# Weight rows moved by 64 bytes, and sample tokens handled in blocks of heads, in a one-core decoder step

## The chip, the core and the metric

The kernel runs on one core of a Trainium2 chip. The metric is the device time of one execution in microseconds (us); the times of a kernel are several executions of it, and the profile is one more, taken by the hardware profiler. The engines are TensorE (matmuls; its weight loads have a row of their own in the profile, PEld), VectorE (DVE), ScalarE (ACT), GpSimd (POOL) and SyncE (SP), whose queue issues all DMA transfers here. The memory beside the engines is SBUF, 128 partitions of bytes; the matmuls write to PSUM, in banks.

## The reference

One layer of a hybrid decoder for 256 prompt tokens and 8 sample tokens (one new token of each of eight sequences), width 2048, all in float32:

```python
xn = rmsnorm(x, norm1_g)
z_u, z_v, q, k, v, g = split(xn @ w_in)              # 2048 x 6144, six parts of 1024 columns
z_v = layernorm(gelu(z_v), sgu_norm_g)               # 8 heads of 128 channels
out_a = gelu(z_u) * (tril(W_s) z_v + b)              # per head, over positions in chunks of 128
out_b = silu(g) * groupnorm(retention(rot(q), rot(k), v, state)) * ret_gn_g   # 8 heads of 128
h = x + concat(out_a, out_b) @ w_out
h = h + cross_attention(rmsnorm(h, norm2_g), memory) # w_cq; w_ck, w_cv of 256 memory tokens; w_co
h = h + relu(rmsnorm(h, norm3_g) @ w_ff1)**2 @ w_ff2 # 2048 -> 8192 -> 2048
y = rmsnorm(h, final_norm_g)
```

A sample token is alone in its chunk: its position mixing is one number per head, W_s[0, 0], and its bias is b[0]. Its retention reads and updates a stored 128 x 128 state per head. The outputs are y, the memory's keys and values, the retention states of prompt and samples, and the samples' layer-normed v.

## The kernel before

**Layout.** Activations lie transposed: 128 features on the partitions, 264 tokens (T; 8 samples first, then the prompt) along the free dimension. A float32 matmul is made of three matmuls in the type fp32r: each operand is split into a high part (a rounded copy) and a low part (the rest), and a product is high x high + high x low + low x high. In the profile the three are lines 163 (weights high, activation high), 164 (weights high, activation low) and 165 (weights low, activation high). These three in a row are called a triple here.

**Weights.** All weights come as chunks of 256 x 512 numbers, two rows of 128 x 512 side by side in one tile [128, 2, 512]; `chunks` is the list of them in order. For each chunk SP loads `w` (five buffers), ScalarE copies it to the high part `wh` (line 1071) and VectorE subtracts for the low part `wl` (line 1079), four buffers each, two chunks ahead of TensorE. Row k of the tile (0 "even", 1 "odd") begins k x 2048 bytes into it. `group_act` takes a chunk with four accumulators of 128 output columns (m) and both rows k: eight triples, 24 matmuls, with 264 columns of activations streaming (256 for `w_ck`, where the memory streams). `group_mem` (`w_cv`) has the roles exchanged: memory tokens as the loaded operand and 512 columns of weights streaming. `group_last` holds the last four chunks of `w_ff2`, sorted by m.

**Activation rows.** `rows` makes tiles [128, 2, 576] for four rows of 264 numbers, and `row(t, k)` finds row k at 272 x (k mod 2) columns, 1088 bytes, in half k // 2; halves are 2304 bytes apart. They sit in 26 slots ("s") of one size, 4608 bytes. The memory's operands are tiles [128, 4, 256] with rows of 1024 bytes.

**Order of work.** Everything else is written as generators. `run_point` is called after every two triples: it advances every `chain` that is due, then the first due task of `tasks` (one per point, with lanes that keep order), then issues due stores (`store`, ten points after the call unless said otherwise). The instructions of each engine stand in the order in which this emits them.

**Around the change.** The order of the input projection is v, q, k, q, k, v, vA, vA, g, g, u, u, with 8 chunks each. `retention(h)` runs for eight heads in two lanes: transposes of k and v, scores, the state product `pp` and its copy `so` (line 647, one buffer) with a store, ScalarE's scaling of the old sample states (line 649), and four steps on VectorE in which `st` is updated and multiplied with the queries into `rs_t` [128, 8] (lines 658 and 660). Then the prompt's products `rp` and a transpose of `rs_t` to 8 partitions, the group norm of both (`s1`, `s2`, cleared by two memsets on VectorE, lines 672 and 673, and filled by ScalarE's accumulating operations, lines 675 and 682), and three transposes back, one of them of the 8 sample rows. `spatial(h)` does the position mixing of a head: a matmul on 8 partitions with a small diagonal matrix `dg` for the samples (line 486), two on 128 partitions for the prompt (line 488), and VectorE's scaling and bias for each. `sample_attn` is the samples' cross-attention. The tag "t" has nine buffers of 264 numbers that many steps share (`t264`), "sm" 24 small ones, "ms" three PSUM banks (`misc`), "mm" five (`bank`).

Of the kernel before, what the change touches and what calls it, by code (L numbers as in the profile page):

```python
# [42 lines left out]
def _emit(tc, cst, wpool, spool, tpool, psum, dpool, I, O):  # L43
# [21 lines left out]

    def small(n, name):
        return tpool.tile([128, n], F32, name=name, tag="sm", bufs=24)
# [28 lines left out]
    w00 = cst.tile([8, 8], F32, name="w00")  # L96
# [24 lines left out]
    def group_last(w, opnd, evict):  # L121
        st = {}

        def mm(ci, hi, lo):
# [3 lines left out]
            for m in R4:  # L128
                ps = bank([128, T], "acc")
                for i in range(8):  # L130
                    xh, xl = opnd(i)
                    h, l = st[i // 2]
                    a = h[:, i % 2, m * 128:(m + 1) * 128]
                    b = l[:, i % 2, m * 128:(m + 1) * 128]
# [39 lines left out]
    def group_mem(w, opnd, evict):  # L174
        st = {}

        def mm(ci, hi, lo):
            if ci == 0:
                st["ps"] = [bank([128, 512], "acc") for _ in range(2)]
            for tq in range(2):  # L180
                for k in range(2):
# [5 lines left out]
                    pe.matmul(ps, lhsT=a, rhs=hi[:, k, :], start=(kt == 0), stop=False)  # L187
                    pe.matmul(ps, lhsT=a, rhs=lo[:, k, :], start=False, stop=False)  # L188
                    pe.matmul(ps, lhsT=b, rhs=hi[:, k, :], start=False, stop=(kt == 15))  # L189
# [182 lines left out]
    def sgu_loads():  # L372
# [5 lines left out]
        sp.dma_start(out=w00[:], in_=I["w00"].partition_broadcast(8))  # L378
# [36 lines left out]
    def ev_vA(g):  # L415
        def ev(ps):
            z = normed(ps)
            ge = slot([128, 4, T], "ge")
            if g == 0:
                sgu_loads()  # L420
                S["vn"] = [slot([128, 1024], "vn0"), slot([128, 1024], "vn1"), None]
                S["vns"] = slot([8, 1088], "vns")
                S["vn"][2] = S["vns"][:, 0:1024]
# [11 lines left out]
            def gen():  # L435
# [4 lines left out]
                else:  # L440
                    chain(layernorm(), 12)
                    for h in range(8):
# [29 lines left out]
    def masks():  # L472
        gp.tensor_tensor(out=S["wst"][:], in0=S["wst"][:], in1=trilt.unsqueeze(1).broadcast_to([128, 8, 128]),
                         op=ALU.mult)
        dg = S["vns"][:, 1024:1088].rearrange("p (h b) -> p h b", h=8)
        gp.tensor_tensor(out=dg, in0=ident[0:8, 0:8].unsqueeze(1).broadcast_to([8, 8, 8]),
                         in1=w00[:].unsqueeze(2).broadcast_to([8, 8, 8]), op=ALU.mult)
        S["dg"] = dg
        yield
        S["spat"] = [slot([128, 4, T], "spat") for _ in range(2)]  # L480

    def spatial(h):
        vn = S["vn"]
        c = slice(h * 128, (h + 1) * 128)
        ps = misc([128, T], "spp")
        pe.matmul(ps[:, 0:8], lhsT=vn[2][:, c], rhs=S["dg"][:, h, :], start=True, stop=True)
        for q in range(2):
            pe.matmul(ps[:, 8 + 128 * q:136 + 128 * q], lhsT=vn[q][:, c], rhs=S["wst"][:, h, :],  # L488
# [4 lines left out]
            in0=ps[:, 8:T].rearrange("p (q i) -> p q i", q=2), scalar=gain(G_SGU, h),  # L493
# [76 lines left out]
    def retentions(g):  # L570
        if g == 0:
            S["state"] = {}
            load_state(0)
            load_state(1)
        for h in range(4 * g, 4 * g + 4):
# [33 lines left out]
    def retention(h):  # L609
# [8 lines left out]
        kn = S["rpool"].tile([128, 384], F32, name="kn", tag="kn", bufs=2)  # L618
# [27 lines left out]
        so = S["rpool"].tile([128, 128], F32, name="so", tag="so", bufs=1)  # L646
        act.copy(so[:], pp[:])
        store(O["state_p"][h], so[:])
        act.activation(st[:], st[:], AF.Copy, scale=GAMMA[h])
        yield 2  # L650
        rs_t = S["rpool"].tile([128, 8], F32, name="rs_t", tag="rs_t", bufs=2)
# [11 lines left out]
        store(O["state_s"][h], st[:])  # L663
        yield 2
        rp = misc([128, 3, 128], "rp")
# [7 lines left out]
        dve.memset(s2[:], 0.0)  # L673
        for i, (c0, n) in enumerate(TOK):
            act.activation(rn[0:n, i * 128:(i + 1) * 128], rp[0:n, i, :], AF.Copy, accum_out=s1[0:n, i:i + 1])

        def norm():
            nm = small(3, "gnm")
            dve.tensor_scalar(out=nm[:], in0=s1[:], scalar1=-1.0 / 128, scalar2=None, op0=ALU.mult)
            yield 2  # L680
            for i, (c0, n) in enumerate(TOK):
                act.activation(jk[0:n, i * 128:(i + 1) * 128], rn[0:n, i * 128:(i + 1) * 128], AF.Square,
                               bias=nm[0:n, i:i + 1], accum_out=s2[0:n, i:i + 1])
            yield
            va, rs = small(3, "gva"), small(3, "grs")
            dve.tensor_scalar(out=va[:], in0=s2[:], scalar1=1.0 / 128, scalar2=EPS, op0=ALU.mult, op1=ALU.add)
            rsqrt(rs[:], va[:], 3)
            yield 2
            for i, (c0, n) in enumerate(TOK):
                y = rn[0:n, i * 128:(i + 1) * 128]  # L690
                dve.tensor_scalar(out=y, in0=y, scalar1=nm[0:n, i:i + 1], scalar2=rs[0:n, i:i + 1],
# [3 lines left out]
        tp = misc([128, T], "tp")  # L695
        for i, (c0, n) in enumerate(TOK):
            transpose(tp[:, c0:c0 + n], rn[0:n, i * 128:(i + 1) * 128])
        act.activation(vt, tp[:], AF.Copy, scale=halfgn[:, h:h + 1])
        done.add(h)

    def ev_g(g):
        def ev(ps):
# [3 lines left out]
            def gen():  # L706
# [4 lines left out]
                assert done.issuperset(range(4 * g, 4 * g + 4))  # L711
# [133 lines left out]
    def sample_attn(h):  # L845
# [6 lines left out]
        sc = small(16, "scs")  # L852
# [23 lines left out]
        so = S["mpool"].tile([128, 4, 8], F32, name="so", tag="so", bufs=4)  # L876
# [191 lines left out]
    def emit_hi(i):  # L1068
        hi = wpool.tile([128, 2, 512], F32R, name="wh", tag="wh", bufs=N_CAST)
        for k in (slice(0, 1), slice(1, 2)) if i < FINE else (slice(0, 2),):  # L1070
            act.copy(hi[:, k, :], raws[i][:, k, :])  # L1071
# [178 lines left out]
```

## Time and profile before

| | |
|---|---|
| median of 3 runs | 1579.33 us (1578.64 to 1582.74) |
| profiled execution, its own time | 1581.44 us |
| its span, first to last instruction | 1579.6 us |
| TensorE busy, matmuls | 1563.9 us, 12515 matmuls |
| VectorE busy | 1037.8 us |
| ScalarE busy | 747.9 us |
| GpSimd busy | 122.4 us |
| DMA | 334.61 MB, 212 GB/s in the mean |
| granted TensorE clock | 0.998 |

In rows of the profile, "L164 PE MATMUL acc<-rl,wh 128*128 128x264 f32 x128 | 36.0, 281" reads: line 164, TensorE, a matmul from tiles rl and wh into acc, 128 rows by 128 columns of weights, 264 columns streamed, 128 of them, 36.0 us busy in sum, 281 ns the mean of one. Matmuls overlap, so a matmul lasts longer than the interval to the next one's start. Rows in the order of time have start (us), length (us), and then the same; "[0.79 <-DVE ra L538]" is idle time before it and what ended it. Rows of waits have who waited for whom, the sum in us, how often, and the longest.

### The profile page before, as it was taken

The page shows a single profiled execution, that of the slowest core. Times are in us where ns is not written, and L with a number is a line of the kernel's source. Part 1 is how long each engine was busy: PE and PEld are TensorE (multiplying, and loading weights), DVE is VectorE, ACT ScalarE, POOL GpSimd, SP SyncE. Part 2 cuts the span into 40 slices and gives each one's busy share as a digit, 9 for nine tenths or more (in the row PEclk, how much of TensorE's full clock was granted, in tenths as well). Part 3 has the DMA queues.
Part 4 walks back from the last instruction along what each step waited for, and adds up shares of the span by engine and source line. Part 5 has one row for each costly group of instructions (what it writes and reads, how often), then busy time and mean ns, then how long its engine had stood idle before and what let it go on. Part 6 is the DMA issues. An engine that isn't in the chain of part 4 may idle for free.

```text
span 1579.6 us, 30820 instructions
## 1 busy us (share of the span) xinstructions
PE 1563.9 (99%) x12515; PEld 1537.5 (97%) x12515; DVE 1037.8 (66%) x1875; ACT 747.9 (47%) x1165; POOL 122.4 (8%) x111
## 2 busy tenths in 40 slices
PE   9999999999999999999999999999999999999997
PEld 8999999999999998899999999999999999999997
DVE  6677688778668777876665555655555465555555
ACT  7445566357544444444454543534444343444443
POOL 0332122110011201010000000000000000000000
PEclk9999999999999999999999999999999999999999
DMA  7677876466578888876555555555655656555552
GB/s 288 193 269 257 281 238 204 154 190 228 185 259 312 298 282 294 310 250 249 182 180 187 183 177 188 174 188 173 189 185 176 190 171 192 179 185 187 171 187 88
DMA packets 98927, 334.61 MB, mean 212 GB/s; under 512 B 11152, under 2 KB 16336, under 8 KB 98784
## 3 DMA queue, kind: packets, MB, share of 16 engines
q1 hardware_dynamic: 98784, 332.64, 63.1%
q8 instruction: 98, 1.61, 0.4%
q14 instruction: 45, 0.37, 0.1%
HBM read 321.42 MB, written 11.17 MB: 211 GB/s over the span
## 4 chain that ended last, share of the span: by engine, by line
issue 47%; PE 47%; DVE 2%; DMA 2%; ACT 0%; SPq 0%; POOL 0%; DVEq 0%; ACTq 0%; POOLq 0%
PE acc L163 13%; PE acc L165 13%; PE acc L164 12%; PE acc L187 2%; PE acc L189 2%; PE acc L188 2%; DMA out_state_p_dram<-so 1%; DVE wl L1079 1%; DMA w<-in_w_in_dram 1%; PE tp L107 1%; PE qb L858 0%; DVE state L658 0%; DVE bkq L660 0%; PE spp L488 0%; DMA bkq<-kqd 0%
## 5 line engine op out<-in xcount | busy, mean ns | idle before, releaser
L1071 ACT CAST wh<-w 128x1024 fp32r<-128x1024 f32 (+1 forms) x513 | 536.0, 1046 | 683.4 <-PE acc L164 596.6
L1079 DVE TENSOR_TENSOR wl<-w,wh 128x1024 fp32r<-128x1024 f32 (+1 forms) x513 | 626.3, 1233 | 256.3 <-ACT wh L1071 255.7
L165 PE MATMUL acc<-h2h,wl 128*128 128x264 f32 x1024 | 290.9, 284 | 0.0
L163 PE MATMUL acc<-h2h,wh 128*128 128x264 f32 x1024 | 290.6, 284 | 0.0
L164 PE MATMUL acc<-h2l,wh 128*128 128x264 f32 x1024 | 288.1, 281 | 0.0
L165 PE MATMUL acc<-rh,wl 128*128 128x264 f32 x992 | 281.8, 284 | 0.0
L163 PE MATMUL acc<-rh,wh 128*128 128x264 f32 x992 | 281.3, 284 | 0.0
L164 PE MATMUL acc<-rl,wh 128*128 128x264 f32 x992 | 279.1, 281 | 0.0
L163 PE MATMUL acc<-xh,wh 128*128 128x264 f32 x768 | 224.9, 293 | 3.9 <-DVE vt L566 1.9
L165 PE MATMUL acc<-xh,wl 128*128 128x264 f32 x768 | 218.8, 285 | 0.4 <-DVE wl L1079 0.2
L164 PE MATMUL acc<-xl,wh 128*128 128x264 f32 x768 | 216.6, 282 | 0.1
L165 PEld LDWEIGHTS acc<-h2h,wl 128*128 128x128 f32 x1024 | 192.5, 188 | 0.0
L164 PEld LDWEIGHTS acc<-h2l,wh 128*128 128x128 f32 x1024 | 192.4, 188 | 0.0
L163 PEld LDWEIGHTS acc<-h2h,wh 128*128 128x128 f32 x1024 | 192.3, 188 | 0.0
L165 PEld LDWEIGHTS acc<-rh,wl 128*128 128x128 f32 x992 | 186.5, 188 | 0.0
L164 PEld LDWEIGHTS acc<-rl,wh 128*128 128x128 f32 x992 | 186.4, 188 | 0.0
L163 PEld LDWEIGHTS acc<-rh,wh 128*128 128x128 f32 x992 | 186.3, 188 | 0.0
L163 PEld LDWEIGHTS acc<-xh,wh 128*128 128x128 f32 x768 | 145.3, 189 | 5.9 <-DVE vt L566 2.1
L164 PEld LDWEIGHTS acc<-xl,wh 128*128 128x128 f32 x768 | 145.5, 189 | 0.3 <-DVE xl L115 0.3
L165 PEld LDWEIGHTS acc<-xh,wl 128*128 128x128 f32 x768 | 145.0, 189 | 0.9 <-DVE wl L1099 0.4
L989 DVE TENSOR_TENSOR hT<-hT,acc 128x264 f32<-128x264 f32 x124 | 53.2, 429 | 71.6 <-PE acc L165 71.6
L103 POOL TENSOR_TENSOR msr<-msv,neghalf 128x3 f32<-128x3 f32 (+1 forms) x5 | 7.8, 1561 | 975.9 <-DVE msv L279 731.8
(249 smaller groups left out, 2740.1 us busy)
## 6 DMA issues: line engine op xcount, KB each, us to landing
w<-in_w_ff_dram SPq DMA_DIRECT2D x256, 512.0 KB, 3.8
w<-in_w_in_dram SPq DMA_DIRECT2D x95, 512.0 KB, 4.1
w<-in_w_out_dram SPq DMA_DIRECT2D x32, 512.0 KB, 3.9
w<-in_w_cq_dram SPq DMA_DIRECT2D x32, 512.0 KB, 4.2
kv<-in_kN_dram SPq DMA_DIRECT2D x32, 512.0 KB, 5.3
kv<-in_vT_dram SPq DMA_DIRECT2D x32, 512.0 KB, 5.0
w<-in_w_ck_dram SPq DMA_DIRECT2D x32, 512.0 KB, 5.7
w<-in_w_cv_dram SPq DMA_DIRECT2D x32, 512.0 KB, 4.6
```

The source lines that it names most:

```text
L103: gp.tensor_tensor(out=out, in0=in_, in1=neghalf[0:in_.shape[0], 0:n], op=ALU.pow)
L107: pe.transpose(out, in_, ident[0:p, 0:p])
L163: pe.matmul(ps, lhsT=a, rhs=xh, start=(i == 0), stop=False)
L164: pe.matmul(ps, lhsT=a, rhs=xl, start=False, stop=False)
L165: pe.matmul(ps, lhsT=b, rhs=xh, start=False, stop=(i == nk - 1))
L187: pe.matmul(ps, lhsT=a, rhs=hi[:, k, :], start=(kt == 0), stop=False)
L188: pe.matmul(ps, lhsT=a, rhs=lo[:, k, :], start=False, stop=False)
L189: pe.matmul(ps, lhsT=b, rhs=hi[:, k, :], start=False, stop=(kt == 15))
L989: dve.tensor_tensor(out=h[m], in0=h[m], in1=ps[m][:], op=ALU.add)
L1071: act.copy(hi[:, k, :], raws[i][:, k, :])
L1079: dve.tensor_tensor(out=lo[:, k, :], in0=raw[:, k, :], in1=hi[:, k, :].bitcast(F32), op=ALU.subtract)
```

## The change

There are two parts.

1. The high and low weight tiles become [128, 1088] (`wcol`). Row k begins at column 528 k, 2112 bytes, so that the odd row begins 64 bytes further modulo 256 than before. The casts write both rows through one access pattern with a gap (`both`), the matmuls read `half_of(t, k)`. Raw tiles `w` and activation rows stay.
2. Sample tokens are taken out of the per-head steps. `spatial_s` transposes the eight heads' samples into one PSUM tile and scales and biases them in four VectorE operations, with `w00` now loaded to 128 partitions and multiplied by the gain; `spatial(h)` keeps the prompt alone. `sample_norm(g)` does the group norm of four heads' samples on 32 partitions, after the last of them; `retention(h)` keeps the prompt's two blocks. For room in SBUF `so` of retention moves to the "t" buffers, `scs` to buffers of its own, the result of `sample_attn` into `q8[h]`, and `kn` and `vns` shrink.

```diff
+    def wcol(name):
+        return wpool.tile([128, 1088], F32R, name=name, tag=name, bufs=N_CAST)
+
+    def half_of(t, k):
+        return t[:, 528 * k:528 * k + 512]
+
+    def both(t):
+        return t[:, 0:1056].rearrange("p (k f) -> p k f", k=2)[:, :, 0:512]
...
-                a = hi[:, k, m * 128:(m + 1) * 128]
-                b = lo[:, k, m * 128:(m + 1) * 128]
+                a = half_of(hi, k)[:, m * 128:(m + 1) * 128]
+                b = half_of(lo, k)[:, m * 128:(m + 1) * 128]
...
-        sp.dma_start(out=w00[:], in_=I["w00"].partition_broadcast(8))
+        sp.dma_start(out=w00[:], in_=I["w00"].partition_broadcast(128))
...
+                    defer(spatial_s(), 56)
                     for h in range(8):
                         defer(spatial(h), 56)
...
-        gp.tensor_tensor(out=dg, in0=ident[0:8, 0:8].unsqueeze(1).broadcast_to([8, 8, 8]),
-                         in1=w00[:].unsqueeze(2).broadcast_to([8, 8, 8]), op=ALU.mult)
-        S["dg"] = dg
+        gp.tensor_tensor(out=w00[:], in0=w00[:], in1=gcol[:, G_SGU:G_SGU + 8], op=ALU.mult)
...
+    def spatial_s():
+        ps = misc([128, 64], "sps")
+        for h in range(8):
+            transpose(ps[:, 8 * h:8 * h + 8], S["vn"][2][:, h * 128:(h + 1) * 128])
+        for g in range(2):
+            hs = slice(4 * g, 4 * g + 4)
+            o = S["spat"][g][:, :, 0:8]
+            dve.tensor_tensor(out=o, in0=ps[:, 32 * g:32 * g + 32].rearrange("p (h b) -> p h b", h=4),
+                              in1=w00[:, hs].unsqueeze(2).broadcast_to([128, 4, 8]), op=ALU.mult)
+            dve.tensor_tensor(out=o, in0=o, in1=S["bbc"][:, hs, 0:1].broadcast_to([128, 4, 8]), op=ALU.add)
+        yield
...
-        pe.matmul(ps[:, 0:8], lhsT=vn[2][:, c], rhs=S["dg"][:, h, :], start=True, stop=True)
...
-        dve.tensor_scalar(out=o[:, 0:8], in0=ps[:, 0:8], scalar1=gain(G_SGU, h),
-                          scalar2=S["bbc"][:, h, 0:1], op0=ALU.mult, op1=ALU.add)
...
-        so = S["rpool"].tile([128, 128], F32, name="so", tag="so", bufs=1)
-        act.copy(so[:], pp[:])
+        so = t264("so")[:, 0:128]
+        act.copy(so, pp[:])
...
+        S["left"][g] -= 1
+        if not S["left"][g]:
+            defer(sample_norm(g), 4)
...
-        transpose(rp[0:8, 2, :], rs_t[:])
...
-        s1, s2 = small(3, "gs1"), small(3, "gs2")
-        dve.memset(s1[:], 0.0)
-        dve.memset(s2[:], 0.0)
-        for i, (c0, n) in enumerate(TOK):
-            act.activation(rn[0:n, i * 128:(i + 1) * 128], rp[0:n, i, :], AF.Copy, accum_out=s1[0:n, i:i + 1])
+        s1, s2 = small(2, "gs1"), small(2, "gs2")
+        for i in range(2):
+            act.activation(rn[:, i * 128:(i + 1) * 128], rp[:, i, :], AF.Copy, accum_out=s1[:, i:i + 1])
...
-        tp = misc([128, T], "tp")
-        for i, (c0, n) in enumerate(TOK):
-            transpose(tp[:, c0:c0 + n], rn[0:n, i * 128:(i + 1) * 128])
-        act.activation(vt, tp[:], AF.Copy, scale=halfgn[:, h:h + 1])
+        tp = misc([128, 256], "tp")
+        for i in range(2):
+            transpose(tp[:, i * 128:(i + 1) * 128], rn[:, i * 128:(i + 1) * 128])
+        act.activation(vt[:, 8:T], tp[:], AF.Copy, scale=halfgn[:, h:h + 1])
...
+    def sample_norm(g):
+        rp = misc([32, 128], "rps")
+        transpose(rp[:], S["rs_t"][g][:])
+        x = half("rns")[0:32, 0:128]
+        s1, s2, nm, va, rs = [small(1, "gss")[0:32, :] for _ in range(5)]
+        act.activation(x, rp[:], AF.Copy, accum_out=s1)
...
+        chain(norm(), 2)
+        yield 16
+        tp = misc([128, 32], "tps")
+        transpose(tp[:], x)
+        dve.tensor_tensor(out=S["v"][g][:, :, 0:8], in0=tp[:].rearrange("p (m b) -> p m b", m=4),
+                          in1=halfgn[:, 4 * g:4 * g + 4].unsqueeze(2).broadcast_to([128, 4, 8]), op=ALU.mult)
+        done.add(8 + g)
...
-        so = S["mpool"].tile([128, 4, 8], F32, name="so", tag="so", bufs=4)
+        so = q8[h]
...
-        hi = wpool.tile([128, 2, 512], F32R, name="wh", tag="wh", bufs=N_CAST)
-        for k in (slice(0, 1), slice(1, 2)) if i < FINE else (slice(0, 2),):
-            act.copy(hi[:, k, :], raws[i][:, k, :])
+        hi = wcol("wh")
+        if i < FINE:
+            for k in range(2):
+                act.copy(half_of(hi, k), raws[i][:, k, :])
+        else:
+            act.copy(both(hi), raws[i][:])
```

`emit_lo` changes in the same way as `emit_hi`, and `group_last`, `group_mem` and the first chunk read and write through `half_of`.

More of the change, by code (lines that the diff above doesn't have):

```diff
@@ L95, in _emit @@
     sel = cst.tile([128, 8], F32R, name="sel")
-    w00 = cst.tile([8, 8], F32, name="w00")
+    w00 = cst.tile([128, 8], F32, name="w00")
     halfgn = cst.tile([128, 8], F32, name="halfgn")
@@ L186, in mm @@
                     ps = st["ps"][tq][:]
-                    pe.matmul(ps, lhsT=a, rhs=hi[:, k, :], start=(kt == 0), stop=False)
-                    pe.matmul(ps, lhsT=a, rhs=lo[:, k, :], start=False, stop=False)
-                    pe.matmul(ps, lhsT=b, rhs=hi[:, k, :], start=False, stop=(kt == 15))
+                    pe.matmul(ps, lhsT=a, rhs=half_of(hi, k), start=(kt == 0), stop=False)
+                    pe.matmul(ps, lhsT=a, rhs=half_of(lo, k), start=False, stop=False)
+                    pe.matmul(ps, lhsT=b, rhs=half_of(hi, k), start=False, stop=(kt == 15))
                     yield
@@ L484, in spatial @@
         c = slice(h * 128, (h + 1) * 128)
-        ps = misc([128, T], "spp")
-        pe.matmul(ps[:, 0:8], lhsT=vn[2][:, c], rhs=S["dg"][:, h, :], start=True, stop=True)
+        ps = misc([128, 256], "spp")
         for q in range(2):
-            pe.matmul(ps[:, 8 + 128 * q:136 + 128 * q], lhsT=vn[q][:, c], rhs=S["wst"][:, h, :],
+            pe.matmul(ps[:, 128 * q:128 * q + 128], lhsT=vn[q][:, c], rhs=S["wst"][:, h, :],
                       start=True, stop=True)
@@ L571, in retentions @@
         if g == 0:
-            S["state"] = {}
+            S["state"], S["rs_t"], S["left"] = {}, {}, {}
             load_state(0)
             load_state(1)
+        S["left"][g] = 4
         for h in range(4 * g, 4 * g + 4):
@@ L645, in retention @@
             pe.matmul(pp[:], lhsT=kn[:, c], rhs=vn[:, c], start=(i == 0), stop=(i == 1))
-        so = S["rpool"].tile([128, 128], F32, name="so", tag="so", bufs=1)
-        act.copy(so[:], pp[:])
-        store(O["state_p"][h], so[:])
+        so = t264("so")[:, 0:128]
+        act.copy(so, pp[:])
+        store(O["state_p"][h], so)
         act.activation(st[:], st[:], AF.Copy, scale=GAMMA[h])
         yield 2
-        rs_t = S["rpool"].tile([128, 8], F32, name="rs_t", tag="rs_t", bufs=2)
+        if g not in S["rs_t"]:
+            S["rs_t"][g] = S["rpool"].tile([128, 32], F32, name="rs_t", tag="rs_t", bufs=2)
+        rs_t = S["rs_t"][g][:, 8 * m:8 * m + 8]
         for b0 in range(0, 8, 2):
@@ L710, in gen @@
                 yield
-                assert done.issuperset(range(4 * g, 4 * g + 4))
+                assert done.issuperset([*range(4 * g, 4 * g + 4), 8 + g])
                 for m in R4:
@@ L1068, in emit_hi @@
     def emit_hi(i):
-        hi = wpool.tile([128, 2, 512], F32R, name="wh", tag="wh", bufs=N_CAST)
-        for k in (slice(0, 1), slice(1, 2)) if i < FINE else (slice(0, 2),):
-            act.copy(hi[:, k, :], raws[i][:, k, :])
+        hi = wcol("wh")
[4 more added lines that the diff above has]
+            act.copy(both(hi), raws[i][:])
         his[i] = hi
     def emit_lo(i):
-        lo = wpool.tile([128, 2, 512], F32R, name="wl", tag="wl", bufs=N_CAST)
+        lo = wcol("wl")
         hi = his.pop(i)
         raw = raws.pop(i)
-        for k in (slice(0, 1), slice(1, 2)) if i < FINE else (slice(0, 2),):
-            dve.tensor_tensor(out=lo[:, k, :], in0=raw[:, k, :], in1=hi[:, k, :].bitcast(F32), op=ALU.subtract)
+        if i < FINE:
+            for k in range(2):
+                dve.tensor_tensor(out=half_of(lo, k), in0=raw[:, k, :], in1=half_of(hi, k).bitcast(F32),
+                                  op=ALU.subtract)
+        else:
+            dve.tensor_tensor(out=both(lo), in0=raw[:], in1=both(hi).bitcast(F32), op=ALU.subtract)
         casts[i] = (hi, lo)
```

50 lines of the change are left out of this document (28 added, 22 removed).

## The prediction

> **What bounds the kernel now.** I read the page's first part, then busy time by stretches, then starts of single matmuls in the order of time, then the waits of each engine. TensorE has no slack: from 830 to 1555 us it is busy for the whole of the time, while VectorE and ScalarE work about half of it.
>
> ```profile
> PE 1563.9 (99%) x12515; PEld 1537.5 (97%) x12515; DVE 1037.8 (66%) x1875; ACT 747.9 (47%) x1165; POOL 122.4 (8%) x111
> ```
>
> ```profile
> 85.00:270.00 185.00, 181.64 (x1473) 178.34 (x1472) 146.29 (x390) 106.29 (x253) 43.67 (x40) 0.99 0.75 255
> 830.00:1555.00 725.00, 725.00 (x6017) 725.00 (x6016) 405.88 (x512) 314.88 (x396) 1.77 (x1) 1.00 0.56 181
> ```
>
> (Columns: length, then busy time and count of TensorE, its weight loads, VectorE, ScalarE, GpSimd, clock, DMA.) So whatever changes the interval from one matmul's start to the next, or puts fewer instructions on TensorE, moves the end one for one; what VectorE, ScalarE or a queue gains counts only where TensorE waits for it, and that is between 85 and 270 us.
>
> The interval is not the same everywhere. These are starts of the first matmul of a weight chunk at both ends of two undisturbed stretches, then the count of matmuls between (each count has the two that hang over the ends):
>
> ```profile
> 326.77 0.28 PE L163 MATMUL acc<-mgh,wh 128*128 128x264 f32 x1
> ...
> 372.85 0.28 PE L163 MATMUL acc<-mgh,wh 128*128 128x264 f32 x1
> ...
> 1045.34 0.28 PE L163 MATMUL acc<-rh,wh 128*128 128x264 f32 x1
> ...
> 1161.07 0.28 PE L163 MATMUL acc<-h2h,wh 128*128 128x264 f32 x1
> ```
>
> ```profile
> 326.77:372.85 46.08, 46.08 (x386) 1.00 0.67 221
> 1045.34:1161.07 115.73, 115.73 (x962) 1.00 0.57 183
> ```
>
> 46.08 us over 384 is 120.00 ns; 115.73 us over 960 is 120.55 ns. Both stretches run the same code with operands at the same places modulo 256. Which matmul has the excess shows in the length of the second matmul of a triple (L164), here of two successive triples at 1051 us, the even operand row and then the odd one:
>
> ```profile
> L164 PE MATMUL acc<-rl,wh 128*128 128x264 f32 x1 | 0.3, 279 | 0.0
> ```
>
> ```profile
> L164 PE MATMUL acc<-rl,wh 128*128 128x264 f32 x1 | 0.3, 284 | 0.0
> ```
>
> From 300 to 390 us both rows have the short one, 278 ns in the mean; from 1000 to 1090 us, where 279 and 284 alternate, it is 281:
>
> ```profile
> L164 PE MATMUL acc<-mgl,wh 128*128 128x264 f32 x96 | 26.7, 278 | 0.0
> ...
> L164 PE MATMUL acc<-mul,wh 128*128 128x264 f32 x80 | 22.3, 278 | 0.0
> ...
> L164 PE MATMUL acc<-xl,wh 128*128 128x264 f32 x75 | 20.9, 278 | 0.0
> ```
>
> ```profile
> L164 PE MATMUL acc<-rl,wh 128*128 128x264 f32 x128 | 36.0, 281 | 0.0
> ```
>
> The odd row begins 272 x 4 = 1088 bytes behind the even one, 64 modulo 256; its weights 2048 bytes behind, 0 modulo 256. The even row and its weights agree modulo 256, the odd ones don't. The excess falls on the odd row, as it must if the relation matters.
>
> **Part 1: the weight tiles.** Weights of odd rows move by 64 bytes. If the odd row then runs like the even one, six matmuls cost 720.0 instead of 723.3 ns. The chunk list has 448 chunks of 264 columns, 24 matmuls each: 10752. The 96 + 80 + 75 triples just shown, 753 matmuls, are at 120.00 already, so 10000 x 0.55 ns = 5.5 us. What loses: the memory operand has rows of 1024 bytes, all at an even place, so the odd weights of w_ck and w_cv stop agreeing with it: 128 + 64 pairs of rows x 3.3 ns = 0.6 us at the most, and nothing at the least, since 256 columns are fewer; I take 0.3. And each third matmul of a triple now runs while weights at the other row's place are loaded; its price isn't in the trace (the odd rows have it with all three), so bounds: nothing, or the odd row's whole excess again, which cancels the 5.5. I take nothing, because in the odd triple it is the second matmul that is long.
>
> One rule speaks against this part. The Trainium skill, TensorE: Matmul & The Clock Gate (Step-by-step: what each phase is for), says that TensorE reads weights and moving operand through two independent SBUF ports, so that loading the next weights takes nothing from the running matmul. By that rule the relation of the two addresses is worth 0. The trace agrees as far as 120.00 ns occurs with disagreeing addresses; it doesn't with the 279 and 284.
>
> The casts now write two runs of 512 with a gap, in one instruction still:
>
> ```profile
> L1071 ACT CAST wh<-w 128x1024 fp32r<-128x1024 f32 (+1 forms) x513 | 536.0, 1046 | 683.4 <-PE acc L164 596.6
> L1079 DVE TENSOR_TENSOR wl<-w,wh 128x1024 fp32r<-128x1024 f32 (+1 forms) x513 | 626.3, 1233 | 256.3 <-ACT wh L1071 255.7
> ```
>
> VectorE's is 1.23 us and ScalarE's 1.05 per chunk of 24 x 120.55 ns = 2.89 us; the trace has no such cast, so bounds: nothing, or as much again per run as half a cast, 0.6 us, which VectorE could still hide. I take nothing, being nearest to the same number of elements. VectorE is fullest from 85 to 270 us (146 of 185), and if that cover is gone, each late cast stops TensorE.
>
> **Part 2: sample tokens in blocks, on TensorE.** Instructions on 8 partitions are dear. A spatial head, against the retention product that has the same four passes:
>
> ```profile
> 291.62 0.28 PE L165 MATMUL acc<-xh,wl 128*128 128x264 f32 x1
> 291.84 0.38 PE L486 MATMUL spp<-vns 8*128 8x8 f32 x2
> 292.15 0.71 PE L488 MATMUL spp<-wst,vn 128*128 128x128 f32 x4
> ...
> 292.82 0.28 PE L164 MATMUL acc<-xl,wh 128*128 128x264 f32 x1
> ```
>
> ```profile
> 233.66 0.28 PE L165 MATMUL acc<-xh,wl 128*128 128x264 f32 x1
> 233.78 0.61 PE L645 MATMUL pp<-vn,kn 128*128 128x128 f32 x4
> ...
> 234.35 0.29 PE L164 MATMUL acc<-xl,wh 128*128 128x264 f32 x1
> ```
>
> 1.20 against 0.69 us: the 8-row product costs 0.51 us, eight times 4.1. The last transposes of a head, three with one on 8 rows, against a pair:
>
> ```profile
> 214.66 0.29 PE L165 MATMUL acc<-xh,wl 128*128 128x264 f32 x1
> 214.78 0.54 PE L107 MATMUL tp<-cmat,kn 128*128 128x128 f32 x3
> ...
> 215.48 0.29 PE L164 MATMUL acc<-xl,wh 128*128 128x264 f32 x1
> ```
>
> ```profile
> 217.42 0.28 PE L165 MATMUL acc<-xh,wl 128*128 128x264 f32 x1
> 217.54 0.38 PE L107 MATMUL tp<-cmat,k 128*128 128x128 f32 x2
> ...
> 217.88 0.28 PE L164 MATMUL acc<-xl,wh 128*128 128x264 f32 x1
> ```
>
> 0.82 against 0.46: 0.36 us, eight times 2.9. The pair itself is 0.46 less two intervals of 0.12, so a full-row transpose is 0.11; eight of rs_t go, 0.9. Added: sample_norm twice, a full-row transpose and one on 32 rows, which I price like 8 rows: 2 x 0.47 = 0.9. spatial_s, eight transposes on 8 rows: the first 0.36, each more the second pass of the spatial product, 0.51 - 0.36 = 0.15: 1.4 (between 0.4, were the seven free, and 2.9, were each a first). Net 4.1 + 2.9 + 0.9 - 0.9 - 1.4 = 5.6 us, bounds 4.1 to 6.6.
>
> **Part 2: waits.** Between 85 and 270 us TensorE stops three times:
>
> ```profile
> 130.90 0.28 PE L165 MATMUL acc<-xh,wl 128*128 128x264 f32 x1
> 131.97 0.39 PE L163 MATMUL acc<-xh,wh 128*128 128x264 f32 x1 [0.79 <-DVE ra L538]
> ...
> 159.82 0.28 PE L165 MATMUL acc<-xh,wl 128*128 128x264 f32 x1
> 161.96 0.47 PE L163 MATMUL acc<-xh,wh 128*128 128x264 f32 x1 [1.86 <-DVE vt L566]
> ```
>
> ```profile
> 199.59 0.28 PE L668 MATMUL rp<-vn,sm 128*128 128x128 f32 x1
> 200.56 0.27 PE L107 MATMUL rp<-cmat,rs_t 128*8 128x128 f32 x1 [0.70 <-DVE bkq L660]
> ```
>
> Less an ordinary interval these are 0.95, 2.02 and 0.86 us. Behind them stand ScalarE's waits:
>
> ```profile
> ACT kn L675 <- DVE gs L673: 20.8, 6, 5.2
> ...
> ACT so L647 <- DMA out_state_p_dram<-so: 12.3, 3, 5.8
> ```
>
> The first is for memsets of s1 and s2, queued on VectorE behind the state updates; they go, and the copy of z that the first stop needs is queued behind that wait. The third stop is the rs_t transpose, which leaves that place. The second stop's vt is queued behind state updates that ScalarE released late, after waiting for the store of so. so moves into the nine "t" buffers. Counted in order, the second pair of heads gets different buffers; in the first and third pair eight other tiles lie between, so the ninth is the same buffer again and that wait stays. All three stops lose their cause: 3.8 us. Bounds: 0, if VectorE is merely late elsewhere, to 3.8. Next late would be the ge transposes after the third pair's store. One wait is added: sample_norm's first transpose needs the last state update of four heads, and the weight matmuls queue behind it; it comes four points (2.9 us) later instead of two, so I take 0 for it, and at most 0.86 twice, as the third stop. VectorE also loses 16 memsets and 8-row operations, ScalarE 16 short ones; hidden, but in the fullest stage. w00 goes to 128 partitions instead of 8, one small load on SP's queue, needed a dozen points later; GpSimd's mask is as small as before. Both free.
>
> **The sum.** 5.5 - 0.3 + 5.6 + 3.8 = 14.6 us. The profiled execution took 1581.4 us (span 1579.6), 2.1 over the median of 1579.33; where it lost these 2.1 nothing shows. From the one 1566.8, from the other 1564.7; I say 1566.
>
> **Rivals.** (1) The places modulo 256 do nothing: both speeds occur with the same addresses, a matter of phase that settles at either. For it: the 120.00 ns stretch, and w_ck, where all places agree and L164 is no shorter than its neighbours:
>
> ```profile
> L164 PE MATMUL acc<-meml,wh 128*128 128x256 f32 x58 | 16.4, 283 | 0.0
> L163 PE MATMUL acc<-memh,wh 128*128 128x256 f32 x58 | 16.4, 283 | 0.0
> ```
>
> Against: odd and even differ steadily at 1051 us. Then 9.4 us less: 1571. By the Trainium skill's rule above this is the case. (2) Part 1 gives nothing and the stops merely move, ScalarE's store waits of the first and third pair still holding up casts: 5.6 less, 1575. Against it: two of the three causes are taken out, not shifted. (3) The price moves to the third matmul: in each of the 1792 pairs two matmuls run while weights 64 bytes off are loaded. If each lost the time of 64 bytes of moving row, 16 columns, by 120 ns / 264 that is 7.3 ns, 14.5 per pair less the 3.3 gained: 20 us, and 20 - 9.4 gives 1590, slower. It decides from 5.2 ns net per pair. Against it: today's odd rows have the offset on all three and pay 3.3 per pair.
>
> **Numbers.** The forecast has 0.52, its own range 1563 to 1569; rival 1 has 0.27, rival 2 0.13, rival 3 0.05, the rest 0.03 for waits in the new blocks. The range, 1562 to 1575, reaches through rival 1 to the edge of rival 2. A measurement here can tell 0.3%, 4.7 us: forecast, rival 1 and about half of rival 2 are faster by more, 0.86; 0.09 the same; 0.05 slower.
>
> **What would show it.** Right: chunk starts 2.880 us apart after 830 us, L164 at 278 to 279 ns in every group; no 8-row product at the spatial heads, bursts of 0.69 there; no wait of ScalarE for gs; TensorE busy throughout 85 to 270 us. Wrong: L164 still at 281 (rival 1); L165 or L163 longer (rival 3); stops with the same releasers at 131 or 160 us (rival 2).

## The result and the profile after

| | before | after |
|---|---|---|
| median | 1579.59 us (6 runs) | 1589.2 us (6 runs, 1586.58 to 1591.28) |
| ratio, 95% interval | | 1.0056, 1.0044 to 1.0069 |
| span of the profiled execution | 1579.6 us | 1589.0 us |
| forecast | | 1566 us, 1562 to 1575 |

The change makes the kernel 9 to 10 us slower. TensorE is as full as before; from 830 to 1555 us it only gets through fewer matmuls, 5935 where it was 6017. First the engine totals of the profile after, then busy time by stretches:

```profile
PE 1573.5 (99%) x12495; PEld 1548.5 (97%) x12495; DVE 1035.2 (65%) x1855; ACT 744.8 (47%) x1141; POOL 121.8 (8%) x113
```

```profile
85.00:270.00 185.00, 182.17 (x1476) 180.05 (x1475) 147.21 (x375) 105.65 (x230) 43.90 (x43) 0.99 0.76 257
830.00:1555.00 725.00, 725.00 (x5935) 725.00 (x5934) 399.37 (x503) 309.10 (x390) 1.77 (x1) 1.00 0.55 180
```

The lines 163, 164 and 165 of a triple are 172, 173 and 174 now. Starts of the first matmul of a chunk at both ends of two stretches of after, 29 and 40 chunks apart:

```profile
746.05 0.28 PE L172 MATMUL acc<-oh,wh 128*128 128x264 f32 x1
...
829.57 0.28 PE L172 MATMUL acc<-h2h,wh 128*128 128x264 f32 x1
...
1047.54 0.29 PE L172 MATMUL acc<-rh,wh 128*128 128x264 f32 x1
...
1164.88 0.29 PE L172 MATMUL acc<-h2h,wh 128*128 128x264 f32 x1
```

A chunk has four times six matmuls (an even triple and an odd one). The first stretch has 83.52 us over 116 sixes, 720.0 ns; the second 117.34 over 160, 733.4 by these rounded starts and 733.3 by those of the trace. Before had two paces, 720.0 and 723.3; after has 720.0 in this one stretch and 733.3 nearly everywhere else, with weight tiles and operand rows at the same places modulo 256 in both. The second stretch is the slow one, and it is where before ran at 723.3. The groups from 1000 to 1090 us, first before and then after, show which matmul is longer:

```profile
L165 PE MATMUL acc<-rh,wl 128*128 128x264 f32 x128 | 36.4, 284 | 0.0
L163 PE MATMUL acc<-rh,wh 128*128 128x264 f32 x128 | 36.3, 284 | 0.0
```

```profile
L172 PE MATMUL acc<-rh,wh 128*128 128x264 f32 x128 | 36.7, 287 | 0.0
L174 PE MATMUL acc<-rh,wl 128*128 128x264 f32 x128 | 36.4, 284 | 0.0
L173 PE MATMUL acc<-rl,wh 128*128 128x264 f32 x128 | 36.1, 282 | 0.0
```

High x high went from 284 to 287, high x low, which was to fall to 278, from 281 to 282. By the starts of all matmuls in that stretch, the even triple went from 359.7 to 365.9 ns and the odd one from 363.6 to 367.5: the even row, whose addresses kept their places, lost more than the odd row, whose weights moved. Summed stage by stage over the starts of all weight matmuls in both traces, the pace cost 14.7 us: 252 chunks of the feed-forward layers x 4 x 10.0 ns = 10.1, and 4.6 in the stages before. The stage of `w_cv`, where the weights stream, took 1.0 us more.

The bursts of part 2 came out as forecast. A spatial head and the last transposes of a head in after, in the order of time:

```profile
290.69 0.28 PE L174 MATMUL acc<-xh,wl 128*128 128x264 f32 x1
290.81 0.61 PE L505 MATMUL spp<-wst,vn 128*128 128x128 f32 x4
291.18 0.37 PE L172 MATMUL acc<-xh,wh 128*128 128x264 f32 x1
291.38 0.28 PE L173 MATMUL acc<-xl,wh 128*128 128x264 f32 x1
```

```profile
214.50 0.29 PE L174 MATMUL acc<-xh,wl 128*128 128x264 f32 x1
214.63 0.38 PE L116 MATMUL tp<-cmat,kn 128*128 128x128 f32 x2
...
214.97 0.28 PE L173 MATMUL acc<-xl,wh 128*128 128x264 f32 x1
```

0.69 us where it was 1.20, and 0.47 where it was 0.82. Over all such places, with what `spatial_s` (0.8 us with one ordinary interval in it, so 0.7 where 1.4 was forecast) and `sample_norm` add, TensorE saves 6.0 us; 5.6 was forecast.

The stops are another matter. TensorE's waits between 85 and 270 us in after, and the two places in the order of time:

```profile
PE tp L116 <- DVE ge L421: 1.6, 1, 1.6
PE acc L172 <- DVE vt L581: 1.2, 1, 1.2
```

```profile
159.43 0.28 PE L174 MATMUL acc<-xh,wl 128*128 128x264 f32 x1
160.89 0.39 PE L172 MATMUL acc<-xh,wh 128*128 128x264 f32 x1 [1.17 <-DVE vt L581]
...
199.76 0.28 PE L174 MATMUL acc<-xh,wl 128*128 128x264 f32 x1
201.66 1.51 PE L116 MATMUL tp<-cmat,ge 128*128 128x128 f32 x4 [1.61 <-DVE ge L421]
202.82 0.57 PE L172 MATMUL acc<-xh,wh 128*128 128x264 f32 x1
```

The stop at 131 us and that of `rs_t` are gone, 0.95 and 0.86 us. The one for `vt` lost 0.7 of its 2.0. In their place the transposes of `ge` wait: from the last matmul ahead of that burst to the first behind it are 3.06 us, where they were 0.91 before. Net 0.3 us of 3.8.

A stop can cost more than its length. Here are 3.2 us behind the stop for `vt` before and 3.2 us behind the stop for `ge` in after (the last three columns are granted clock, DMA share and GB/s):

```profile
162.20:165.40 3.20, 3.20 (x16) 3.20 (x16) 3.10 (x12) 1.16 (x6) 0.00 (x0) 0.50 0.58 180
```

```profile
202.80:206.00 3.20, 3.20 (x15) 3.20 (x16) 3.06 (x13) 0.92 (x5) 0.00 (x0) 0.50 0.42 138
```

For 3.4 us the granted clock was 0.50 and matmuls started every 0.22 us instead of 0.12, which is 1.5 us lost in each of the two executions. It doesn't follow every such stop: in run 1 below TensorE waits 1.8 us for `vt` and the clock stays at 1.00.

ScalarE's waits show that the causes did go, and what came:

```profile
ACT sm L700 <- DVE gnm L697: 10.1, 4, 5.2
...
ACT so L663 <- DMA out_state_p_dram<-so: 4.4, 1, 4.4
```

No wait for `gs` is left, and that for the store of `so` fell from 12.3 us in 3 times to 4.4 once. Together: 14.7 + 1.0 - 6.0 - 0.3 = 9.4 us, the difference between the spans; the 1.5 us of slow clock stand on both sides.

### The profile page after: what moved, and what is told of

Same layout as the page of the kernel before. It is cut to its first block, busy times and chain, and to the rows that moved or that the text cites. A ratio compares the mean times of both kernels' runs of the same rounds, so it can differ in the third digit from the quotient of the medians.

```text
span 1589.0 us, 30730 instructions
## 1 busy us (share of the span) xinstructions
PE 1573.5 (99%) x12495; PEld 1548.5 (97%) x12495; DVE 1035.2 (65%) x1855; ACT 744.8 (47%) x1141; POOL 121.8 (8%) x113
## 4 chain that ended last, share of the span: by engine, by line
PE 49%; issue 47%; DMA 2%; DVE 1%; POOL 0%; SPq 0%; ACT 0%; DVEq 0%; ACTq 0%; POOLq 0%
PE acc L172 13%; PE acc L174 13%; PE acc L173 13%; PE acc L196 2%; PE acc L197 2%; PE acc L198 2%; DMA w<-in_w_in_dram 1%; PE tp L116 1%; PE qb L900 0%; DVE wl L1128 0%; DMA out_state_p_dram<-so 0%; DMA bkq<-kqd 0%; DVE state L676 0%; PE op L1000 0%; PE pb L923 0%
## 5 line engine op out<-in xcount | busy, mean ns | idle before, releaser
L1116 ACT CAST wh<-w 128x1024 fp32r<-128x1024 f32 x509 | 532.9, 1047 | 702.3 <-PE acc L173 630.3
L1128 DVE TENSOR_TENSOR wl<-w,wh 128x1024 fp32r<-128x1024 f32 x509 | 624.1, 1237 | 260.2 <-ACT wh L1116 259.9
L172 PE MATMUL acc<-h2h,wh 128*128 128x264 f32 x1024 | 294.0, 287 | 0.0
L172 PE MATMUL acc<-rh,wh 128*128 128x264 f32 x992 | 284.7, 287 | 0.0
```

The source lines that it names most:

```text
L172: pe.matmul(ps, lhsT=a, rhs=xh, start=(i == 0), stop=False)
L1116: act.copy(both(hi), raws[i][:])
L1128: dve.tensor_tensor(out=both(lo), in0=raw[:], in1=both(hi).bitcast(F32), op=ALU.subtract)
```

## Experiments

Each kernel is told as a difference from after; paces are ns per six matmuls. "(a, b)" is how far the even and the odd weight row lie from their operand rows modulo 256, in steps of 64 bytes: before is (0, -1), after (0, 0).

**1. Part 2 alone.** The odd weight row goes back to 2048 bytes.

```diff
-        return t[:, 528 * k:528 * k + 512]
+        return t[:, 512 * k:512 * k + 512]
```

> The changed kernel with part 2 alone: the odd weight row back at 2048 bytes (tiles still 4352 bytes apart, so there is room as in the change). All theories: the bursts and stops of the sample blocks as in the changed kernel, some 6 us less TensorE work than before. Theory A (the loss is the places of the weights, an excess of 13.3 ns per six matmuls against 720.0): pace back to 723.3 ns per six, time 1572 to 1575 us. Rival B (the loss comes from the blocks: a disturbance of the order that leaves TensorE in a slow rhythm): pace stays near 733.3, time 1587 to 1591.

Measured: 1571.73 us, ratio 0.9955 (0.9939 to 0.9972). The same pair of chunks as above:

```profile
1035.56 0.28 PE L172 MATMUL acc<-rh,wh 128*128 128x264 f32 x1
...
1151.29 0.28 PE L172 MATMUL acc<-h2h,wh 128*128 128x264 f32 x1
```

115.73 us, 723.3 again. So part 2 gives 7.5 us by the medians (7.1 by the ratio), and part 1 costs 17.5. The two profiled executions lie 19.2 us apart, 15.5 of it in the pace of the weight matmuls; run 1 also waits only 0.6 us for `ge` and has no stretch at the clock of 0.50. The loss lies in the places of the weights, in one way or another.

**2. All triples of the even row first, then those of the odd row**, in every chunk: two changes of row in a chunk instead of eight.

```diff
-            if len(started) < FINE:
-                started.append(1)
-                turns.sort(key=lambda t: t[1])
+            turns.sort(key=lambda t: t[1])
```

> The changed kernel with one edit: every chunk of 264 columns does its four even triples first and then its four odd ones, so the matmuls that run while weights at the other row's place are loaded fall from eight to two per chunk. Theory A1 (the price is paid at the change of rows): the excess of 13.3 ns per pair falls to a quarter, pace near 723.3 ns per six, time 1571 to 1575 us. Rival A2 (each triple has its price by its own two addresses, wherever it stands): 733.3 and 1587 to 1591. Rival C (several steady rhythms exist for the same addresses, 720.0 and 733.3 among them, and which one holds is an accident): single stretches at either, time anywhere from 1568 to 1590.

Measured: 1586.71 us, ratio 1.0045 (1.003 to 1.006).

```profile
1044.15 0.28 PE L170 MATMUL acc<-rh,wh 128*128 128x264 f32 x1
...
1161.21 0.28 PE L170 MATMUL acc<-h2h,wh 128*128 128x264 f32 x1
```

117.06 us over 160 is 731.6, where 733.3 was. So the price doesn't sit at the change of rows.

**3 and 4. Two other places.** Odd weights 128 bytes further than before, (0, 1), with `528` made `544`; and both rows 64 bytes further, (1, 0):

```diff
-        return t[:, 528 * k:528 * k + 512]
+        return t[:, 16 + 512 * k:16 + 512 * k + 512]
```

> The changed kernel with the odd weight row 128 bytes instead of 64 past a multiple of 256, so it lies 64 bytes ahead of its operand row, where before the change it lay 64 behind. Theory A1 (price at the change of rows, by how far the two rows' weights differ): worse than the change, above 740 ns per six and above 1595 us. Rival A2 (price by the distance of a triple's own addresses, whatever its sign): like before the change, 723.3 and 1572 to 1575 us.

> The changed kernel with both weight rows 64 bytes later and no gap between them: the odd weights agree with their operand row, the even ones lie 64 bytes ahead of theirs; no step between the weight rows, as before the change. Theory A1 (price at a step between the weight rows): like part 2 alone, 723.3 ns per six, 1572 to 1575 us. Rival A2 (a triple's own addresses): odd rows cheap, even rows dear, in sum between 720 and 730. Rival D (only the operand row's own place counts): the odd row stays the dear one, 723.3.

Measured: 1579.1 us, ratio 1.0002 (0.9991 to 1.0012), and 1586.24, ratio 1.0045 (1.0029 to 1.0061). The pair of chunks, first (0, 1), then (1, 0):

```profile
1040.74 0.28 PE L172 MATMUL acc<-rh,wh 128*128 128x264 f32 x1
...
1157.00 0.28 PE L172 MATMUL acc<-h2h,wh 128*128 128x264 f32 x1
```

```profile
1042.60 0.29 PE L172 MATMUL acc<-rh,wh 128*128 128x264 f32 x1
...
1159.93 0.29 PE L172 MATMUL acc<-h2h,wh 128*128 128x264 f32 x1
```

726.6 (726.7 without the rounding of the starts) and 733.3: every theory then in hand missed. (1, 0) has both weight rows alike and disagrees on the even row; (0, 0) agrees on both; they run alike. No rule of the kind "agreement is fast" or "the step between weight rows costs" gives 723.3, 733.3, 726.7 and 733.3. One stage did gain in the second kernel: against the 256 memory columns (`w_ck`), six matmuls took 688.8 ns in the mean of their intervals, 711.1 in after and 717.7 before. In the groups, after and then (1, 0):

```profile
L173 PE MATMUL acc<-meml,wh 128*128 128x256 f32 x256 | 72.1, 282 | 0.0
```

```profile
L173 PE MATMUL acc<-meml,wh 128*128 128x256 f32 x256 | 71.1, 278 | 0.0
```

**5 and 6. The same addresses, disturbed.** What was left was the stretch of after at 720.0. So one more matmul went ahead of every eighth chunk, 8, 16, 24 ... columns wide, into a PSUM bank that nobody reads; once in after, once in part 2 alone.

```diff
+                if j == 0 and n == T:
+                    kicked.append(1)
+                    f = len(kicked) - KICK0
+                    if f >= 0 and f % 8 == 0:
+                        w = 8 * (f // 8 % 33 + 1)
+                        kt = misc([128, w], "kick")
+                        pe.matmul(kt[:], lhsT=a, rhs=xh[:, 0:w], start=True, stop=True)
```

> The changed kernel; from the 193rd chunk of 264 columns on, every eighth chunk has one more matmul ahead of its first, of 8, 16, 24 and so on columns up to 256, into a bank that nobody reads. Addresses stay. Theory P (the places alone set the pace): each stretch between two extra matmuls runs at 733.3 ns per six, with at most one or two exceptions, and the run takes some 2 to 4 us longer than the changed kernel, 1591 to 1593. Theory Y (one layout has several steady rhythms, and the phase between weight loads and moving reads at the start of a stretch chooses): at least a quarter of the 25 to 30 stretches run at another pace, 720.0 among them, the change standing exactly at an extra matmul, and the time is 1580 to 1589.

> Part 2 alone (odd weights back at 2048 bytes), with the same extra matmuls. Theory P: 723.3 ns per six between all of them, 1574 to 1576 us. Theory Y: at least a quarter of the stretches run at 720.0 or another pace than 723.3; were all at 720.0 for half the time, 1571 to 1574 us.

Measured: 1590.26 and 1573.83 us (one run each). In part 2 alone 16 of the 32 stretches between extra matmuls ran at 720.0 and 16 at 723.3, each steady up to the next extra matmul, with no address changed. In after three of the 32 went to 720.0 and the others ran at 733.3. Starts of chunks in after, with the extra matmul of 168 columns:

```profile
1269.78 0.28 PE L180 MATMUL acc<-h2h,wh 128*128 128x264 f32 x1
...
1287.38 0.28 PE L180 MATMUL acc<-h2h,wh 128*128 128x264 f32 x1
...
1290.31 0.24 PE L178 MATMUL kick<-h2h,wh 128*128 128x168 f32 x1
...
1293.30 0.28 PE L180 MATMUL acc<-rh,wh 128*128 128x264 f32 x1
...
1310.58 0.28 PE L180 MATMUL acc<-rh,wh 128*128 128x264 f32 x1
```

Six chunks, 24 sixes, take 17.60 us before it and 17.28 behind it: 733.3 and 720.0. The count that theory Y expected, a quarter of the stretches, is exceeded in the sixth run and missed in the fifth, and the fifth also has one exception more than theory P allowed; the changes stand at the extra matmuls in both, against theory P.

**7 and 8. A map of places.** The last 256 chunks are cut into stretches; each has its weight rows at another pair of places, in the eighth run in another order and twice each. `place` gives the first column of the even row and the columns left free between the rows; where both rows don't fit into one access pattern, the casts write them one by one.

```diff
+    def place(i):
+        f = i - (len(chunks) - 256)
+        return PLACES[min(f // 18, 13)] if f >= 0 else (0, 0)
```

> Both parts; the last 256 chunks are cut into 14 stretches of 18, and each has its weight rows at another pair of places: the even one 0, 64, 128, 192 or 256 bytes behind the start of the tile, and 0 to 256 bytes between the rows. With the distance of weights from operand row in steps of 64 bytes (even, odd), known are (0,-1): 723.3, (0,0): 733.3, (0,1): 726.7, (1,0): 733.3 ns per six. Theory P: those four return at these values, the first and the last stretch but one ((0,-1) and, 256 bytes on, (0,3)) agree with one another, and at least one of the other nine is faster than 720. Theory Y: the known four don't all return (at least one is off by 3 ns or more), or a stretch changes its pace midway.

> As the map before, with 28 stretches of 9 chunks in another order, each pair of places twice; chunks before the last 256 have both weight rows 64 bytes ahead of their rows, distances (1,1), all along. Theory P: each pair's two stretches agree with one another and with the map before within 1 ns. Theory Y: several pairs differ by 3.3 ns or a multiple of it between their stretches. If only the distance from the operand row mattered by its being the same in both rows, (1,1) would run as (0,0) does, 733.3.

Measured: 1580.66 and 1589.59 us (one run each), and by place, from the starts of all matmuls in the two traces:

| (a, b) | run 7 | run 8, both times |
|---|---|---|
| (0, -1) | 723.3 | 720.0 |
| (0, -1), 256 bytes more between the rows | 723.3 | 720.0 |
| (0, 0) | 733.3 | 733.3 |
| (0, 1), (0, 2) | 726.7 | 726.7 |
| (1, 0), (1, 1) | 733.3 | 733.3 |
| (1, 2) | 726.7 | 726.7 |
| (1, 3) | 736.7 | 730.0 |
| (2, 1) | 740.0 | 740.0 |
| (2, 2) | 733.3 | 726.7 |
| (2, 3) | 733.3 | 733.3 |
| (3, 2), (3, 3) | 728.9 | 728.9 |

For (0, -1), 12 chunks of run 7 and six of run 8 (the starts at their ends):

```profile
832.03 0.28 PE L183 MATMUL acc<-h2h,wh 128*128 128x264 f32 x1
...
866.75 0.28 PE L183 MATMUL acc<-h2h,wh 128*128 128x264 f32 x1
```

```profile
1328.96 0.28 PE L183 MATMUL acc<-rh,wh 128*128 128x264 f32 x1
...
1346.24 0.28 PE L183 MATMUL acc<-h2h,wh 128*128 128x264 f32 x1
```

34.72 us over 48 sixes, 723.3; 17.28 over 24, 720.0. The places do count: they repeat, and most keep one pace in both runs. But at four of the 14 places the two runs differ, by 3.3 or 6.7 ns, so neither theory came out whole. The addresses there are the same; what differs is what ran before the stretch, and that it decided which of two rhythms was taken is the likely reading. The second round of run 8 has the order of the first, so that each place but the very first follows the same one both times: that its two visits agree is no test apart. Nothing is below 720.0, and nearly all paces are whole steps of 3.3 ns above it. The place of before, with or without 256 bytes more, is the best of the 14, because its two rhythms are 720.0 and 723.3.

**9 and 10. One extra matmul in all.** If a rhythm, once chosen, stays, one extra matmul early in the feed-forward layers is enough: 184 columns in after, 32 columns in part 2 alone.

> The changed kernel with one more matmul in all, of 184 columns, ahead of a chunk early in the first feed-forward layer, into a bank that nobody reads. With 184 columns the run of extra matmuls went from 733.3 to 720.0 ns per six. Theory P (places alone; the exceptions there were accidents): 733.3 behind it too, 1589 us. Theory Y (the phase chooses among the rhythms of one layout, and a chosen one stays): 720.0 ns from there to the end, some 244 chunks x 4 x 13.3 ns = 13.0 us less: 1576 to 1577 us.

> Part 2 alone (odd weights at 2048 bytes), with one more matmul of 32 columns at the same chunk; with 32 columns that layout went from 723.3 to 720.0. Theory P: 1571.7. Theory Y: 720.0 to the end, 244 x 4 x 3.3 ns = 3.2 us less: 1568.5 us.

Measured: 1588.33 us, ratio 1.0051 (1.0036 to 1.0066), and 1568.84 us, ratio 0.9932 (0.9917 to 0.9948). Part 2 alone came out as theory Y said: 720.0 from that chunk to the end. After stayed at 733.3. Its trace shows why the forecast was too simple: 733.3 has two patterns. The mean intervals of the six are 125.8, 120.0, 120.0, 126.0, 120.0, 121.7 ns in the one and 121.0, 125.8, 126.5, 120.0, 122.8, 117.4 in the other. In run 5, the three extra matmuls that led to 720.0 had all found the second; this one found the first.

**13. Two extra matmuls**, eight chunks apart: 16 columns, which had turned the first pattern into the second, then 184.

```diff
+                    w = {200: 16, 208: 184}.get(len(kicked))
+                    if w:
+                        kt = misc([128, w], "kick")
+                        pe.matmul(kt[:], lhsT=a, rhs=xh[:, 0:w], start=True, stop=True)
```

> The changed kernel with two extra matmuls in all, eight chunks apart: one of 16 columns, then one of 184. The single one of 184 found the pattern 125.8, 120, 120, 126, 120, 121.7 ns and left it; in the run of many, those that led to 720.0 (168, 184, 224 columns) all found the other pattern that also adds to 733.3 (121, 125.8, 126.5, 120, 122.8, 117.4), and one of 16 columns turns the first into the second. Theory Y (a layout has a fixed set of rhythms, and the phase alone chooses): 733.3 in the second pattern for eight chunks, then 720.0 ns for the other 236, 236 x 4 x 13.3 ns = 12.6 us less than 1589.2: 1576 to 1577 us. Theory P (the places set the pace, and 720.0 was an accident that doesn't last): 733.3 throughout, 1589.

Measured: 1575.76 us, ratio 0.9977 (0.9966 to 0.9988). The two extra matmuls, and the pair of chunks of the first fences:

```profile
844.24 0.17 PE L176 MATMUL kick<-h2h,wh 128*128 128x16 f32 x1
...
867.82 0.25 PE L176 MATMUL kick<-h2h,wh 128*128 128x184 f32 x1
...
1043.61 0.28 PE L178 MATMUL acc<-rh,wh 128*128 128x264 f32 x1
...
1158.80 0.28 PE L178 MATMUL acc<-h2h,wh 128*128 128x264 f32 x1
```

115.19 us over 160: 720.0, with every weight and operand where after has them. Two matmuls of 0.17 and 0.25 us whose results nobody reads make the changed kernel 13.4 us faster, and faster than before. So part 1's loss in the feed-forward layers is the rhythm that the stream of matmuls fell into, not a fixed price of the addresses. As far as these runs show, the addresses decide which rhythms there are and how easily the fast one is met: after 3 of 32 extra matmuls in after, after 16 of 32 in part 2 alone.

**11 and 12. A version that beats both.** Part 2 alone, but both weight rows of the 32 chunks of `w_ck` begin 64 bytes later (`place` as in the map); run 12 has the extra matmul of 32 columns as well.

```diff
+    def place(i):
+        return (16, 0) if chunks[i].get("mem") else (0, 0)
```

> Part 2 alone, but the weight tiles of the 32 chunks that run against the 256 memory columns begin 64 bytes later, both rows, as in the run that moved all rows by 64 bytes; all others stay. If the 688.8 ns per six of that run belong to the places of these chunks (theory P with Y), the stage falls from 717.1 to 688.8 and 128 sixes x 28.3 ns = 3.6 us go: 1568.1. If it belonged to the state that the stages before had left (Y alone), 717 stays: 1571.7. A phase that is left behind for the next stage may move it by 3 us either way.

> The two edits before together: part 2, the 32 memory chunks 64 bytes later, and one matmul of 32 columns more. Were both right and independent, 1571.7 - 3.6 - 3.2 = 1564.9 us; if the extra matmul meets another phase than before and leaves 723.3, 1568.1; if neither does anything, 1571.7.

Measured: 1569.67 us, ratio 0.9935 (0.992 to 0.995), and 1564.8 us, ratio 0.9905 (0.9889 to 0.9922). The `w_ck` stage ran at 689.5 in both, so that gain belongs to the places of these chunks (or to a rhythm that they bring with them; it wasn't told apart). Run 11 has 2.1 us of the 3.6 by its median (its wait for `ge` is 1.2 us, that of run 1 0.6); the two together have 6.9 where 6.8 was expected. The pair of chunks in run 12, 115.20 us over 160, 720.0:

```profile
1031.12 0.28 PE L186 MATMUL acc<-rh,wh 128*128 128x264 f32 x1
...
1146.32 0.28 PE L186 MATMUL acc<-h2h,wh 128*128 128x264 f32 x1
```

**14. A tenth buffer of 264 columns**, in part 2 alone, to take away what was left of the wait for the store of `so`.

```diff
-        return wpool.tile([128, 1088], F32R, name=name, tag=name, bufs=N_CAST)
+        return wpool.tile([128, 1024], F32R, name=name, tag=name, bufs=N_CAST)
...
-        return tpool.tile([128, T], F32, name=name, tag="t", bufs=9)
+        return tpool.tile([128, T], F32, name=name, tag="t", bufs=10)
```

> Part 2 alone with weight tiles of 4096 bytes; what that frees holds a tenth buffer of 264 columns. Theory S (the stop at the transposes of ge, near 199 us, is the store of so from the third pair of heads still holding ScalarE and, through it, VectorE): ScalarE's wait for that store, 4.4 us once, goes, and the stop with it, 0.6 to 2.4 us; the pace stays, 1569.5 to 1571. Rival (VectorE is simply late there with its own work): the store's wait goes and the stop stays, 1571.7.

Measured: 1571.49 us (one run). ScalarE's wait for the store in run 1, then all that is left of its waits for `so` in this run, then TensorE's waits from 85 to 270 us:

```profile
ACT so L663 <- DMA out_state_p_dram<-so: 2.9, 1, 2.9
```

```profile
ACT so L663 <- PE pp L661: 15.3, 8, 2.7
```

```profile
PE acc L172 <- DVE vt L581: 1.3, 1, 1.3
PE tp L116 <- DVE ge L421: 0.2, 1, 0.2
```

The store's wait is gone, and the wait for `ge` is 0.2 us where run 1 had 0.6: that is the mechanism of theory S. Its time, 1571 at most, was missed, in part because the 32 chunks of `w_co` ran at 723.3 here and at 720.0 in run 1, which takes 0.4 us back. Other traces with nine buffers bear theory S out: the store's wait and the wait for `ge` are 2.5 and 0.3 us in run 2, 2.9 and 0.6 in run 1, 3.6 and 0.8 in run 5, 4.1 and 1.3 in run 3, 4.4 and 1.6 in after, 5.6 and 1.7 in run 8. In runs 7 and 10, which wait 1.7 us for `ge`, the profile puts waits of 4.6 and 4.7 us ahead of `so` down to a weight matmul instead. The link is in the trace of after: VectorE idles until ScalarE, late from that wait, has scaled the old states, and `ge` stands behind the state updates.

```profile
195.30 0.35 DVE L676 SCALAR_TENSOR_TENSOR state<-bkq,vt,state 128x128 f32<-128x128 f32 x1 [2.88 <-ACT state L665]
```

What holds up `vt`, and why the store took longer in after than in run 1, stays open.

## Why the prediction was wrong

**Part 1, forecast -5.5 + 0.3, measured +14.7 in the pace against before and +15.5 against part 2 alone.** This is the step that failed. It read "the even row and its weights agree modulo 256, the odd ones don't; the excess falls on the odd row" as cause, and gave the loss a bound from the odd row's own excess, 3.3 ns a pair. The loss was 10.0 ns a pair, and the larger part of it fell on the even row, whose places had not changed. Run 4 has agreement on the odd row alone, after has it on both, both run at 733.3, and the place of before, which disagrees, is the best of the map. The bound fell because a pace belongs to the whole loop of six: moving one row changes the set of steady rhythms, and the next can be 13 ns away. The nearest rows gave no bound on that. Runs 2 to 4 each show one rhythm of their layout, so they speak against a simple rule of agreement and don't price a place. The small term for `w_ck` and `w_cv`, 0.3, came out near its size by luck: `w_ck` gained 0.8 us and `w_cv` lost 1.0. By what way a place sets its rhythms stays open.

The view that should have weighed more was in the prediction: 720.0 and 723.3 with the same addresses. Rival 1 drew from it that phase decides and that the places do nothing. The first half is shown by runs 5, 6, 10 and 13; the second isn't, since 10 of the 14 places keep their pace in both maps. The Trainium skill, TensorE: Matmul & The Clock Gate (Step-by-step: what each phase is for), says that loading the next weights takes no SBUF read bandwidth from the running matmul. The prediction took from this that the two addresses are worth 0 to one another. The runs don't bear that out: with the instructions unchanged, weights moved by 64 bytes took the steady pace from 723.3 to 733.3 ns, and `w_ck` from 717.1 to 689.5. Whether read bandwidth has to do with it, or where else it arises, no run shows.

**Rival 3 had the time, 1590, and not the mechanism.** Its price was to fall at the change of rows, on the third matmul. Line 174 has 284 ns, as line 165 had; it is line 172 that grew, from the 284 of line 163; and run 2, with a quarter of the changes, kept 731.6 of 733.3.

**The casts, forecast 0: right.** VectorE's busy time from 85 to 270 us is 147 of 185, as before, and TensorE has no stop for `wl` or `wh` there.

**Part 2 on TensorE, forecast -5.6, measured -6.0: right**, with the two bursts at 0.69 and 0.47 us as worked out, and the eight transposes of `spatial_s` at 0.7 instead of 1.4.

**The stops, forecast -3.8, measured -0.3: wrong, inside its bounds.** The causes named did go, and "next late would be the `ge` transposes" named the place that took over; the sum then should have gone by that sentence. The part of rival 2 on the stops was the better reading: they moved. The prediction also left out what followed the stop for `vt`: the stretch at the clock of 0.50 cost another 1.5 us, which would be most of the 2.1 us of which it said that nothing shows where they went. In run 10 too, the execution with the profile took 1572.11 us where the other three took 1568.47 to 1568.98, and its trace has 3.4 us at 0.50 behind the stop for `vt`.

## What to carry to other kernels

A stream of equal matmuls with a weight load each can settle into several steady rhythms; look for them as exact paces over hundreds of instructions before giving a reason for a few ns. If two paces occur with the same addresses, test the phase first: one small extra matmul takes some 0.2 us and shows whether the pace follows. And here the excess of one instruction of a steady loop gave no bound for what the loop does when an address moves: 3.3 ns became 10.

## What was not expected of the hardware

With 264 columns and a weight load each, six matmuls took 720.0, 723.3, 726.7, 730.0, 733.3, 736.7 or 740.0 ns, depending on places modulo 256 and on what came before, steady until something else came between; only two places gave 728.9, one of them as a mix of 723, 729 and 734. With 256 columns they took 688.8 to 717.7 in the mean. A single matmul of 32 columns moved all chunks behind it, some 245, from 723.3 to 720.0. And a stop of 1.6 to 1.9 us was followed by 3.4 us at a granted clock of 0.50 in before and in after, and by none after 1.8 us in run 1.
